# Row sums of squares from a token-major copy of the input, opening loads in another order, and products issued cell by cell

## Chip, cores and metric

One core of one Trainium2 chip runs the whole kernel. The metric is device time in microseconds (us), the median of several runs. TensorE is called PE here, VectorE DVE, ScalarE ACT, GpSimd POOL, and SyncE, which only issues transfers, SP.

## What is computed

One layer of a streaming encoder over 2048 tokens of width 1024, in float32:

```python
h = rmsnorm(x, norm_mix_pre)             # y = x * rsqrt(mean(x*x) + eps) * g
proj = h @ w_in                          # pool 512 | GLU 2*512 | gate_a 1024 | gate_b 1024
branch_a = pool_mixer(u_pool, ...)       # 4 trailing means, small maps, projection
branch_b = conformer_conv(u_glu, ...)    # GLU, depthwise conv 31, layernorm, silu, projection
merged = sigmoid(g_a) * branch_a + sigmoid(g_b) * branch_b
x = x + rmsnorm(merged @ w_o, norm_mix_post)
f = square(relu(rmsnorm(x, norm_mlp_pre) @ w_up)) @ w_down
x = x + rmsnorm(f, norm_mlp_post)
```

Only the first norm's `mean(x*x)` is computed in another way by the change; the rest is the same arithmetic in another order.

## The kernel before, in words

Activations lie channels on partitions, tokens along the row: a tile `x0[c, t]` is 128 x 1024, for 128-channel pairs c = 0..3 and a token half t = 0, 1 of a block. The 2048 tokens are two blocks b = 0, 1 of 1024. Each float32 operand is cut into a high part (an ACT cast, `wh`, `big`, L221 and L228 in the profile) and a low part (a DVE subtraction of the high part, `wl`, `big`, L122), and each product is three passes: high by high, high by low, low by high. Large products are made of smaller ones in octets with sums and differences of cells (`Octet`; the opening's first GLU octet `o1` is a `Plain`, without sums).

One **product** is 24 matmuls 128x512 into a `glu` (or `ga`, `pool`, `up`, `down`...) tile of two PSUM banks, one bank for each output half q: twelve matmuls for q = 0, then twelve for q = 1 (`product`, `matmuls`, L267 to L296). Its operands are a weight of eight 128x128 blocks and two cells of two 512-column blocks k. The opening's products are numbered P1, P2, ... here in PE's order; P1 to P4 belong to t = 0 of `o1`, P5 and P6 to `o2`, and P7 is the first that `run_first` issues behind the hand-written opening.

A scheduler orders each engine's instructions, but in the opening (`opening`, L1612 to L1688) the order is fixed by hand: `InOrder` chains the instructions of an engine as they are written, `high_priority` puts them first, and `cast_behind` names the ACT instruction behind which the casts of `o1`'s weights for t = 1 may come. The opening starts with `idle(20, ...)`, matmuls of ones whose result nobody reads. `first_half` (L829) issues the first transfers: SP's queue takes x, `load`, and ACT's takes the parameters `cst` and the first weight in halves, `store`. P1 to P4 multiply raw x times the norm's gain (`first_parts`, ACT L809 and DVE L893), since the factor 1/rms of a token can be applied behind them. `FirstNorm` finds that factor for t = 0 (`n0`) and t = 1 (`n1`): four squares on ACT (L767), three additions and a half one on DVE (L119), eight matmuls 128x1 with `inv_d` on PE (L858), eleven small DVE operations for the root (L635 to L698), eight 128x128 matmuls that spread it over partitions (`spread`, L728), and an ACT copy (L870). P5 on take normed cells, which `first_cell` (L873, two DVE operations of 0.74 us a cell, L877) makes.

For block b = 1 the same sums are made between the products of block 0 by `in_stats(1)` (L903): it loads x again, takes the squares on ACT, adds on DVE and sums with eight matmuls for each t.

Weights already loaded are kept in device memory as low parts (`kept<-wl`) and fetched again for block 1.

## Time and profile before

| | us |
|---|---|
| median of 3 runs (2153.32 to 2160.22) | 2156.2 |
| the profiled execution | 2155.09 |
| its span in the trace | 2153.0 |
| PE busy in the span | 2133.3 |
| DVE, ACT, POOL busy | 1667.3, 1040.7, 78.2 |
| start of P7 / of P13 in the span | 47.30 / 80.44 |

The span is what the profiler saw of the execution; the 2.1 us around it are launch and end. An engine's busy time divided by the span is its share; the windows view gives the same by stretches, with the clock granted to PE as a share of 2.4 GHz. In a timeline a row is a run of like instructions with the start, the time they took together and, in brackets, how long the engine stood idle before them and what released it.

### The profile page before, as it was taken

The page shows a single profiled execution, that of the slowest core. Times are in us where ns is not written, and L with a number is a line of the kernel's source. Part 1 is how long each engine was busy: PE and PEld are TensorE (multiplying, and loading weights), DVE is VectorE, ACT ScalarE, POOL GpSimd, SP SyncE. Part 2 cuts the span into 40 slices and gives each one's busy share as a digit, 9 for nine tenths or more (in the row PEclk, how much of TensorE's full clock was granted, in tenths as well). Part 3 has the DMA queues.
Part 4 walks back from the last instruction along what each step waited for, and adds up shares of the span by engine and source line. Part 5 has one row for each costly group of instructions (what it writes and reads, how often), then busy time and mean ns, then how long its engine had stood idle before and what let it go on. Part 6 is the DMA issues. An engine that isn't in the chain of part 4 may idle for free.

```text
span 2153.0 us, 25284 instructions
## 1 busy us (share of the span) xinstructions
PE 2133.3 (99%) x9582; PEld 1768.6 (82%) x9582; DVE 1667.3 (77%) x1637; ACT 1040.7 (48%) x1101; POOL 78.2 (4%) x143
## 2 busy tenths in 40 slices
PE   9999999999999999999999999999999999999998
PEld 7888888888888887888888888888888888888887
DVE  8998788997778878997868795667776657576976
ACT  6444453334543635445564684555663332234751
POOL 1000000000000000000000000000000000120002
PEclk9999999999999999999999999999999999999999
DMA  7688898778997786445697698677898997896977
GB/s 275 242 287 326 322 367 272 242 246 309 332 379 247 267 329 259 171 160 188 249 359 298 241 342 326 245 261 276 314 350 303 353 380 261 333 369 234 301 256 217
DMA packets 173929, 618.39 MB, mean 287 GB/s; under 512 B 19312, under 2 KB 21616, under 8 KB 173808
## 3 DMA queue, kind: packets, MB, share of 16 engines
q1 hardware_dynamic: 142736, 505.80, 64.6%
q0 software_dynamic: 17824, 64.07, 8.4%
q10 hardware_dynamic: 13248, 46.92, 5.5%
q8 instruction: 75, 1.23, 0.2%
q14 instruction: 46, 0.38, 0.1%
HBM read 406.89 MB, written 209.81 MB: 286 GB/s over the span
## 4 chain that ended last, share of the span: by engine, by line
PE 88%; DVE 7%; DMA 3%; issue 1%; ACT 1%; SPq 0%; ACTq 0%; DVEq 0%
PE up L271 25%; PE down L271 22%; PE gb L271 7%; PE wo L271 7%; PE ga L271 6%; PE glu L271 5%; PE rb L271 5%; PE A L271 4%; PE B L271 4%; PE pool L271 2%; DVE tr L119 1%; DVE big L122 1%; DVE y L1015 1%; DVE wl L122 1%; DVE tr L122 1%
## 5 line engine op out<-in xcount | busy, mean ns | idle before, releaser
L271 PE MATMUL up<-big,wh 128*128 128x512 f32 x1792 | 481.4, 390 | 4.6 <-DVE tr L119 3.8
L271 PEld LDWEIGHTS up<-big,wh 128*128 128x128 f32 x1792 | 336.7, 188 | 75.2 <-issue 4.2
L228 ACT CAST wh<-wr 128x1024 fp32r<-128x1024 f32 x196 | 205.9, 1051 | 349.4 <-PE up L271 101.4
L1015 DVE SCALAR_TENSOR_TENSOR y<-v,cst,y 128x1024 f32<-128x1024 f32 x240 | 307.6, 1282 | 3.0
L271 PE MATMUL down<-big,wh 128*128 128x512 f32 x872 | 294.9, 389 | 0.0
L228 ACT CAST wh<-ws 128x1024 fp32r<-128x1024 f32 x128 | 134.7, 1053 | 298.8 <-PE up L271 91.2
L271 PE MATMUL up<-big,wl 128*128 128x512 f32 x896 | 276.2, 389 | 0.0
L271 PE MATMUL down<-big,wl 128*128 128x512 f32 x688 | 212.1, 389 | 0.0
L271 PEld LDWEIGHTS up<-big,wl 128*128 128x128 f32 x896 | 168.4, 188 | 35.0
L271 PE MATMUL down<-tr,wh 128*128 128x512 f32 x504 | 196.2, 389 | 0.5 <-DVE tr L122 0.5
L122 DVE TENSOR_TENSOR wl<-ws,wh 128x1024 fp32r<-128x1024 f32 x120 | 146.6, 1221 | 58.7 <-ACT wh L228 58.4
L271 PEld LDWEIGHTS down<-big,wh 128*128 128x128 f32 x872 | 163.6, 188 | 33.9
L122 DVE TENSOR_TENSOR wl<-wr,wh 128x1024 fp32r<-128x1024 f32 (+1 forms) x121 | 146.3, 1212 | 34.7 <-ACT wh L228 33.4
L122 DVE TENSOR_TENSOR big<-big,big 128x1024 fp32r<-128x1024 f32 (+1 forms) x108 | 130.2, 1221 | 41.0 <-ACT big L1150 17.7
L122 DVE TENSOR_TENSOR tr<-tr,big 128x1024 fp32r<-128x1024 f32 x94 | 112.7, 1221 | 53.0 <-ACT big L1892 40.6
L271 PEld LDWEIGHTS down<-big,wl 128*128 128x128 f32 x688 | 129.2, 188 | 26.8
L271 PE MATMUL wo<-big,wh 128*128 128x512 f32 x480 | 128.5, 390 | 0.0
L271 PE MATMUL glu<-big,wh 128*128 128x512 f32 x464 | 125.1, 391 | 0.7 <-ACT wh L535 0.5
L271 PE MATMUL ga<-big,wh 128*128 128x512 f32 x448 | 120.0, 389 | 0.0
L271 PE MATMUL gb<-big,wh 128*128 128x512 f32 x448 | 119.9, 389 | 0.0
L1892 ACT CAST big<-tr 128x1024 fp32r<-128x1024 f32 x70 | 72.1, 1049 | 97.0 <-DMA tr<-fd 75.0
L271 PEld LDWEIGHTS down<-tr,wh 128*128 128x128 f32 x504 | 94.6, 188 | 20.5 <-DVE tr L122 1.0
(245 smaller groups left out, 3406.7 us busy)
## 6 DMA issues: line engine op xcount, KB each, us to landing
tr<-fd SPq DMA_DIRECT2D x98, 512.0 KB, 7.5
wl<-kept SPq DMA_DIRECT2D x85, 512.0 KB, 5.1
wr<-w_down SPq DMA_DIRECT2D x80, 512.0 KB, 7.8
kept<-wl SPq DMA_DIRECT2D x72, 512.0 KB, 6.1
wr<-w_up SPq DMA_DIRECT2D x64, 512.0 KB, 5.1
wr<-w_in SPq DMA_DIRECT2D x59, 512.0 KB, 5.6
fd<-tr ACTq DMA_DIRECT2D x54, 512.0 KB, 5.2
big<-fd SPq DMA_DIRECT2D x48, 512.0 KB, 6.7
```

The costliest lines, as they stand in the source:

```text
L119: return nc.vector.tensor_tensor(o, a, b, op=ALU.add)
L122: return nc.vector.tensor_tensor(o, a, b, op=ALU.subtract)
L228: nc.scalar.copy(hi[:, :n], src[:, :n])
L271: i = nc.tensor.matmul(ps, w[wp][:, (at + k) * P : (at + k + 1) * P], rhs[k][xp], start=start and n == 0, stop=stop and n == len(order) - ...
L1015: nc.vector.scalar_tensor_tensor(acc, v[:, k : k + TB], wk, acc, op0=ALU.mult, op1=ALU.add)
L1892: nc.scalar.copy(hi, t)
```

## The change

- **Sums of squares.** A second input array `xn` holds x with tokens on partitions, 128 x 1024 to a tile. ACT's Square with `accum_out` sums a token's squares along the row (`token_squares`), so neither DVE nor PE adds anything for them. The opening loads eight such tiles more; `in_stats(1)` loads `xn` in the place of `xt`.
- **Opening.** The first transfers come in another order, the first two x tiles in halves, `cst` in two parts. The idle matmuls are 9 in the place of 20, and 3 later ones are dropped. The first weight half is cast on DVE. Cells of t = 1 get their gain on ACT (two 128x512 operations) and 1/rms by one DVE multiplication. `cast_behind` names a later instruction.
- **Products.** Every product issues its 24 matmuls cell by cell: for each of the two cells four high by high, four with the low x, four with the low weight, in each four two for q = 0 and two for q = 1. The first product has a list of its own, `COMING`.

```diff
@@ constants
+STAIRS = tuple(
+    (q, 2 * c + k, wp, xp)
+    for c in (0, 1) for wp, xp in ((0, 0), (0, 1), (1, 0)) for q in (0, 1) for k in (0, 1)
+)
+COMING = ((0, 0, 0, 0), (0, 0, 1, 0), (1, 0, 0, 0), (0, 0, 0, 1), (0, 1, 0, 0), (0, 1, 1, 0))
...
-IDLE = (4, 5, 3)
+IDLE = (4, 5)
@@ product
-        rhs = cell_rhs(cells)
-        i = [matmuls(half_of(ps, q), w, 4 * q, rhs, start, stop) for q in (0, 1)]
-        mark(i[1])
+        in_order(STAIRS, ps, w, cells, start, stop)
+
+    def in_order(order, ps, w, cells, start, stop):
+
+        rhs, seen = cell_rhs(cells), set()
...
+        for n, (q, k, wp, xp) in enumerate(order):
+            i = nc.tensor.matmul(
+                half_of(ps, q), w[wp][:, (4 * q + k) * P : (4 * q + k + 1) * P], rhs[k][xp],
...
@@ Plain.by_halves, Plain.run
-                nc.scalar.copy(hi[:, s], raw[:, s])
+                (nc.scalar.copy if i else nc.vector.tensor_copy)(hi[:, s], raw[:, s])
...
+            if job == (0, 0, 0):
+                in_order(COMING, self.ps, w, cells, True, False)
@@ token_squares
+    def token_squares(st, g, x):
+
+        nc.scalar.activation(x, x, AF.Square, scale=D**-0.5, accum_out=st[:, g : g + 1])
@@ first_half
-            load_x(0, x0, ORDER_X[:1])
-            store(cst, params)
+            store(cst[:, :C_PSC], params[:, :C_PSC])
...
+            half(load, x0[0, 0], xt[0, 0, 0], 0)
+            half(store, w, w_in[0, 0], 0)
+            half(load, x0[0, 0], xt[0, 0, 0], 1)
+            half(store, w, w_in[0, 0], 1)
+            half(load, x0[1, 0], xt[0, 1, 0], 0)
+            half(load, x0[1, 0], xt[0, 1, 0], 1)
+            o.get(1)
             load_x(0, x0, ORDER_X[2:CPS])
-            for q in (1, 2, 3):
-                o.get(q)
-            load_x(0, x0, ORDER_X[CPS:])
+            o.get(2)
+            load(cst[:, C_PSC:], params[:, C_PSC:])
+            n0.load()
+            o.get(3)
@@ FirstNorm
-        def squares(self):
-            sq = Squares(TR)
...
-        def sums(self):
-            self.st = root_psum()
-            for g in range(G):
-                i = nc.tensor.matmul(
...
+        def load(self):
+            self.x, self.st = [tr() for _ in range(G)], small("st", G)
+            for g, x in enumerate(self.x):
+                load(x, xn[0, self.t, g])
+
+        def squares(self, groups):
+            for g in groups:
+                token_squares(self.st, g, self.x[g])
@@ first_cell
+        if t:
+            first_gain(c, t)
+            mul(two(x), two(x), per_token(r0[t]))
+            return x
@@ in_stats
-            sq = Squares(TR)
-            for c in range(CPS):
+            st = small("st", G)
+            for g in range(G):
                 x = tr()
-                load(x, xt[b, c, t])
+                load(x, xn[b, t, g])
                 yield 1
-                sq.add(x)
...
+                token_squares(st, g, x)
...
-            yield from inv_rms_steps([ss], inv_d, TR, 4, got)
+            yield from spread_steps(root_dve(st), TR, 4, got)
@@ opening
-        idle(20, root_psum())
+        idle(9, root_psum())
...
+            n0.squares(range(G))
...
         o1.run((0, 0, 1), None, none)
         with tc.high_priority(offset=URGENT):
-            n0.sums()
             n0.root()
             o1.prepare(1, 0, 1)
-            act()
             o2.prepare(1)
...
+            n1.load()
+            load_x(0, x0, ORDER_X[CPS:])
+            n1.squares((0, 1))
...
         o1.run((1, 0, 0), None, none)
-        idle(IDLE[2], root_psum(), marks[mybir.EngineType.PE])
         with tc.high_priority(offset=URGENT):
             n0.spread()
-            n1.sums()
             cells0(0, 0), cells0(1, 0)
-            parts.need(1)
-            n1.root()
+            for g in (2, 3):
+                parts.step()
+                n1.squares((g,))
...
         o1.run((1, 0, 1), None, none)
         with tc.high_priority(offset=URGENT):
+            n1.root()
             cells0(2, 0), cells0(3, 0)
+            parts.step()
+            o2.prepare(2)
             parts.need(2)
-            o1.cast_behind = [
...
-            o2.prepare(2)
+            first_gain(0, 1), first_gain(1, 1)
...
         o2.run(1, None, none)
         with tc.high_priority(offset=URGENT):
             n1.spread()
             cells0(0, 1), cells0(1, 1)
             parts.need(8)
+            first_gain(2, 1), first_gain(3, 1)
+            o1.cast_behind = [
...
@@ arrays
+        "xn": g["x"].reshape(NB, 2, T // P, P, D),
```

On SP the first twelve transfers are now these (`big` is x, `wr` a weight of `w_in`, `xn` the second layout, the first two rows two halves each):

```order
L137 DMA big_216<-xt 128x512 x2
L137 DMA big_217<-xt 128x512 x2
L137 DMA wr_224<-w_in 128x1024
L137 DMA big_226<-xt 128x1024
L137 DMA big_228<-xt 128x1024
L137 DMA wr_230<-w_in 128x1024
L137 DMA cst<-params 128x228
L137 DMA tr_233<-xn 128x1024
L137 DMA tr_234<-xn 128x1024
L137 DMA tr_235<-xn 128x1024
L137 DMA tr_236<-xn 128x1024
L137 DMA wr_242<-w_in 128x1024
```

Before, the queue began with four whole x tiles, three weights and the four x tiles of t = 1; these four now stand behind four more `xn` tiles, as rows 18 to 21.

On ACT in the opening, from the cast of the first cell of P6 to the cast of P7's weight; before (`wh_646` is P7's weight, `big_529` and `big_533` P6's cells, `wh_692` the weight after):

```order
L557 COPY tr_523<-glu_420 128x1024
L221 CAST big_529<-big_221 128x1024
L221 CAST big_533<-big_223 128x1024
L228 CAST wh_646<-wr_644 128x1024
L444 COPY tr_569<-glu_544 128x1024
L870 COPY r_239<-rb_571 128x512
L228 CAST wh_692<-wr_690 128x1024
L221 CAST big_585<-big_231 128x1024
L221 CAST big_589<-big_233 128x1024
```

and now (`wh_515` is P6's weight, `wh_630` P7's, `big_509` and `big_520` P6's cells, `big_397` to `big_403` the x tiles of t = 1):

```order
L230 CAST big_509<-big_226 128x1024
L237 CAST wh_515<-wr_513 128x1024
L230 CAST big_520<-big_228 128x1024
L838 ACTIVATE big_397<-big_397,cst 128x512 x2
L838 ACTIVATE big_399<-big_399,cst 128x512 x2
L466 COPY tr_553<-glu_528 128x1024
L901 COPY r_213<-rb_555 128x512
L230 CAST big_567<-big_397 128x1024
L230 CAST big_571<-big_399 128x1024
L838 ACTIVATE big_401<-big_401,cst 128x512 x2
L838 ACTIVATE big_403<-big_403,cst 128x512 x2
L237 CAST wh_630<-wr_628 128x1024
```

P7's weight was cast straight behind P6's cells; it now stands behind the eight gains of t = 1, P7's own cells `big_567` and `big_571`, and two copies.

On DVE in the up projection, ahead of the operation that frees the `up` tile whose owner PE waits for at 847.84 us; before:

```order
L119 TENSOR_TENSOR ws_6664<-wr_6658,wr_6660 128x1024
L122 TENSOR_TENSOR tr_6519<-big_5845,big_5641 128x1024
L122 TENSOR_TENSOR tr_6525<-big_5936,big_5743 128x1024
L122 TENSOR_TENSOR wl_6604<-ws_6601,wh_6603 128x1024
L122 TENSOR_TENSOR big_6522<-tr_6519,big_6521 128x1024
L122 TENSOR_TENSOR big_6528<-tr_6525,big_6527 128x1024
L1015 SCALAR_TENSOR_TENSOR y_6385<-v_5650,cst,y_6385 128x1024
L122 TENSOR_TENSOR ws_6666<-ws_6664,wr_6662 128x1024
L122 TENSOR_TENSOR wl_6669<-ws_6666,wh_6668 128x1024
L119 TENSOR_TENSOR tr_6593<-up_6481,tr_6557 128x1024
```

and now:

```order
L128 TENSOR_TENSOR ws_6624<-wr_6618,wr_6620 128x1024
L131 TENSOR_TENSOR wl_6564<-ws_6561,wh_6563 128x1024
L131 TENSOR_TENSOR tr_6479<-big_5805,big_5601 128x1024
L131 TENSOR_TENSOR tr_6485<-big_5896,big_5703 128x1024
L1057 SCALAR_TENSOR_TENSOR y_6345<-v_5610,cst,y_6345 128x1024
L131 TENSOR_TENSOR big_6482<-tr_6479,big_6481 128x1024
L131 TENSOR_TENSOR ws_6626<-ws_6624,wr_6622 128x1024
L131 TENSOR_TENSOR big_6488<-tr_6485,big_6487 128x1024
L131 TENSOR_TENSOR wl_6629<-ws_6626,wh_6628 128x1024
L128 TENSOR_TENSOR tr_6553<-up_6441,tr_6517 128x1024
```

The sum `ws_6666`, which ACT casts into `wh_6668`, stood directly ahead of `wl_6669`, which needs that cast; the same sum, `ws_6626`, now has a subtraction between it and `wl_6629`.

## Rows read from the trace of the kernel before

**Rows 1.** The page, busy us (share of the span) xinstructions of each engine.

```profile
PE 2133.3 (99%) x9582; PEld 1768.6 (82%) x9582; DVE 1667.3 (77%) x1637; ACT 1040.7 (48%) x1101; POOL 78.2 (4%) x143
```

**Rows 2.** Waits of PE: what it waited for, us in total, times, longest.

```profile
PE pool L271 <- DVE tr L119: 1.5, 2, 1.1
...
PE up L271 <- DVE big L122: 0.8, 1, 0.8
...
PE down L271 <- DVE tr L122: 0.5, 1, 0.5
```

**Rows 3.** Windows: us, busy (x) by engine, granted clock, DMA share, GB/s.

```profile
0.00:5.00 5.00, 4.01 (x11) 3.19 (x12) 0.00 (x0) 1.49 (x2) 1.21 (x10) 1.00 0.59 201
5.00:10.00 5.00, 4.47 (x19) 3.06 (x18) 3.50 (x6) 3.95 (x7) 0.00 (x0) 1.00 1.02 395
8.00:9.00 1.00, 1.00 (x5) 0.79 (x5) 1.00 (x2) 1.00 (x2) 0.00 (x0) 1.00 1.04 416
10.00:15.00 5.00, 5.00 (x24) 4.14 (x23) 4.50 (x6) 5.00 (x7) 0.87 (x2) 1.00 1.04 389
15.00:20.00 5.00, 4.41 (x21) 3.35 (x19) 4.55 (x5) 4.92 (x6) 0.38 (x1) 1.00 1.01 407
...
847.00:851.00 4.00, 3.16 (x8) 2.56 (x9) 4.00 (x4) 2.84 (x3) 0.00 (x0) 0.57 0.54 221
```

**Rows 4.** PE timeline, 0 to 95 us: start, us, operation [idle before <-releaser].

```profile
0.99 6.41 PE L610 MATMUL rb<-ones 128*128 128x512 f32 x20 [0.99 <-POOL inv_d L187]
...
19.97 1.02 PE L858 MATMUL rb<-inv_d,tr 128*128 128x1 f32 x8 [0.59 <-DVE tr L119]
...
26.42 0.85 PE L610 MATMUL rb<-ones 128*128 128x512 f32 x3
...
29.29 1.65 PE L271 MATMUL glu<-big,wh 128*128 128x512 f32 x6
...
47.30 1.52 PE L271 MATMUL glu<-big,wh 128*128 128x512 f32 x6
...
50.02 1.52 PE L271 MATMUL glu<-big,wh 128*128 128x512 f32 x6
...
80.44 1.52 PE L271 MATMUL glu<-big,wh 128*128 128x512 f32 x6
```

**Rows 5.** ACT timeline, 0 to 95 us.

```profile
9.78 2.56 ACT L809 ACTIVATE big<-big,cst 128x512 fp32r<-128x512 f32 x4
...
13.18 3.90 ACT L767 ACTIVATE tr<-big 128x1024 f32<-128x1024 f32 x4
...
22.29 1.07 ACT L767 ACTIVATE tr<-big 128x1024 f32<-128x1024 f32 x1 [0.83 <-DMA big<-xt]
...
40.54 1.04 ACT L228 CAST wh<-wr 128x1024 fp32r<-128x1024 f32 x1
41.48 1.01 ACT L444 COPY tr<-glu 128x1024 f32<-128x1024 f32 x1
42.39 0.58 ACT L870 COPY r<-rb 128x512 f32<-128x512 f32 x1
```

**Rows 6.** DVE timeline, 0 to 33 us and 834 to 850 us.

```profile
15.21 3.89 DVE L119 TENSOR_TENSOR tr<-tr,tr 128x1024 f32<-128x1024 f32 x3 [0.68 <-ACT tr L767]
...
25.40 0.15 DVE L635 TENSOR_SCALAR sa<-rb 128x4 f32<-128x4 f32 x1
...
27.48 2.36 DVE L122 TENSOR_TENSOR wl<-wr,wh 128x1024 fp32r<-128x1024 f32 x2
29.76 2.72 DVE L877 SCALAR_TENSOR_TENSOR big<-big,cst,rb 128x512 f32<-128x512 f32 x4
...
836.13 1.23 DVE L122 TENSOR_TENSOR wl<-ws,wh 128x1024 fp32r<-128x1024 f32 x1 [1.11 <-ACT wh L228]
```

**Rows 7.** PE timeline, 145 to 154 us and 842 to 852 us.

```profile
151.86 0.95 PE L599 MATMUL rb<-inv_d,tr 128*128 128x1 f32 x8
...
847.84 2.90 PE L271 MATMUL up<-big,wh 128*128 128x512 f32 x6 [3.76 <-DVE tr L119]
```

More of the change, by code (lines that the diff above doesn't have):

```diff
@@ L292, in product @@
     def product(ps, w, cells, start=True, stop=True):
-        rhs = cell_rhs(cells)
-        i = [matmuls(half_of(ps, q), w, 4 * q, rhs, start, stop) for q in (0, 1)]
-        mark(i[1])
+        in_order(STAIRS, ps, w, cells, start, stop)
+    def in_order(order, ps, w, cells, start, stop):
+        rhs, seen = cell_rhs(cells), set()
+        last = {q: n for n, (q, k, wp, xp) in enumerate(order)}
+        for n, (q, k, wp, xp) in enumerate(order):
+            i = nc.tensor.matmul(
+                half_of(ps, q), w[wp][:, (4 * q + k) * P : (4 * q + k + 1) * P], rhs[k][xp],
+                start=start and q not in seen, stop=stop and n == last[q],
+                skip_group_check=True,
+            )
+            if not seen:
+                ordered(i)
+            seen.add(q)
+        mark(i)
     def half_of(ps, q):
@@ L549, in run @@
                 self.ps = psum(self.lab)
-            product(self.ps, w, cells, start=k == 0, stop=k == 1)
+            if job == (0, 0, 0):
+                in_order(COMING, self.ps, w, cells, True, False)
+            else:
+                product(self.ps, w, cells, start=k == 0, stop=k == 1)
             flush()
@@ L804, in block_kernel, with gained @@
     ORDER_X = tuple((c, t) for t in (0, 1) for c in (0, 1, 2, 3))
-    def gained(dst, src, gain, c):
-        for i in (0, 1):
+    def gained(dst, src, gain, c, halves=(0, 1)):
+        for i in halves:
             s = slice(i * T, (i + 1) * T)
@@ L829, in first_half, with half @@
     def first_half(o):
+        def half(queue, dst, src, i):
+            queue(dst[:, i * T : (i + 1) * T], src[:, i * T : (i + 1) * T])
         with tc.high_priority(offset=URGENT):
-            load_x(0, x0, ORDER_X[:1])
-            store(cst, params)
+            store(cst[:, :C_PSC], params[:, :C_PSC])
             o.raw[0] = w = mk(p_wr, "wr")
-            store(w[:, :T], w_in[0, 0, :, :T])
-            load_x(0, x0, ORDER_X[1:2])
-            store(w[:, T:], w_in[0, 0, :, T:])
+            for c, t in ORDER_X[:2]:
+                x0[c, t] = mk(*BIG)
+            half(load, x0[0, 0], xt[0, 0, 0], 0)
[5 more added lines that the diff above has]
+            o.get(1)
             load_x(0, x0, ORDER_X[2:CPS])
-            for q in (1, 2, 3):
-                o.get(q)
-            load_x(0, x0, ORDER_X[CPS:])
+            o.get(2)
+            load(cst[:, C_PSC:], params[:, C_PSC:])
+            n0.load()
+            o.get(3)
     class FirstNorm:
@@ L847, in __init__ @@
             self.t, self.r = t, r[:, t * T : (t + 1) * T]
[L849 to L863 removed]
+        def load(self):
[5 more added lines that the diff above has]
+                token_squares(self.st, g, self.x[g])
         def root(self):
[L866 removed]
+            self.dg = spread_dve(root_dve(self.st), None)
         def spread(self):
@@ L871, in spread, with first_gain @@
             r0[self.t] = rb if self.t == 0 else self.r
+    gained_x = set()
+    def first_gain(c, t):
+        if (c, t) not in gained_x:
+            gained_x.add((c, t))
+            gained(x0[c, t], x0[c, t], C_PRE, c)
     def first_cell(c, t):
         x = x0[c, t]
+        if t:
+            first_gain(c, t)
+            mul(two(x), two(x), per_token(r0[t]))
+            return x
         for i in (0, 1):
@@ L888, in first_parts @@
                 hi, lo = mk(*BIG, F32R), mk(*BIG, F32R)
-                with tc.high_priority(offset=URGENT):
-                    gained(hi, x0[c, 0], C_PRE, c)
-                    for i in (0, 1):
+                for i in (0, 1):
+                    with tc.high_priority(offset=URGENT):
+                        gained(hi, x0[c, 0], C_PRE, c, (i,))
                         s = slice(i * T, (i + 1) * T)
@@ L1611, in block_kernel @@
     o1, o2 = glu(0, parts)
-    first_half(o1)
     r = mk(p_ss, "r", F32, (P, W))[:, :TB]
     n0, n1 = (FirstNorm(t, r) for t in (0, 1))
+    first_half(o1)
     dve = InOrder(mybir.EngineType.DVE)
     def opening():
-        act = InOrder(mybir.EngineType.Activation)
-        idle(20, root_psum())
+        fix = InOrder(mybir.EngineType.DVE, mybir.EngineType.Activation)
+        idle(9, root_psum())
         with tc.high_priority(offset=URGENT):
             halves = o1.by_halves(0, 0, 0)
+            next(halves)
             parts.step()
@@ L1626, in opening @@
             drain(halves)
+            o1.prepare(0, 0, 1)
             parts.need(("u", 1))
-            o1.prepare(0, 0, 1)
-            n0.squares()
             o1.prepare(1, 0, 0)
-            n1.squares()
-        dve()
+            n0.squares(range(G))
+        fix()
         o1.run((0, 0, 0), None, none)
@@ L1665, in opening @@
             parts.need(8)
-        dve()
+            first_gain(2, 1), first_gain(3, 1)
+            o1.cast_behind = [
+                i for i in nc.cur_bb.bb.instructions if i.engine == mybir.EngineType.Activation
+            ][-1]
+        fix()
         o2.run(2, None, none)
-        dve.skip()
+        fix.skip()
         with tc.high_priority(offset=URGENT):
@@ L1671, in opening @@
             parts.need(3)
-        dve()
+        fix()
+        dve.last.update(fix.last)
     opening()
```

27 lines of the change are left out of this document (10 added, 17 removed).

## The prediction

> **What bounds the kernel now.** I read the page first: PE is busy for 2133.3 of a span of 2153.0 us [rows 1], so only work taken off PE, or one of the 20 us in which it stands still, can shorten the run. The waits of PE come next: beside 3.76 us at 847.84 for a DVE operation [rows 7], they are 1.5 us in two places ahead of `pool` products (1.1 and 0.44), 0.8 and 0.5 [rows 2]. Then the timeline of the opening, where the change is. PE does 20 idle matmuls to 7.40, eight sums of one column at 19.97 behind a wait of 0.59, and from 26.42 to 29.29, for 2.87 us, idle matmuls, the spread and the second sums instead of a product. P7 starts at 47.30, P13 at 80.44 [rows 4]. A half product of twelve matmuls takes 50.02 - 47.30 = 2.72 us, 0.227 each, so 5.44 a product. The opening is judged by one number: when P12 ends, 80.44 before.
>
> **The opening, step by step.** I replayed it by hand along each engine's new order, with durations from rows. On ACT, start to start (a row's last instruction overlaps the next by about 0.1): a cast 41.48 - 40.54 = 0.94, a copy 42.39 - 41.48 = 0.91, the copy of 1/rms 0.58 - 0.1, a square (3.90 - 0.1)/4 = 0.95, a gain of half a tile (2.56 - 0.1)/4 = 0.62 [rows 5]. On DVE: a whole tile (2.36 - 0.1)/2 = 1.13, a normed half cell 2.72/4 = 0.68, the root 27.48 - 25.40 = 2.1 [rows 6].
>
> Removed: on DVE the additions, twice about 4.5 us (3.89 for three, and a half one) [rows 6]; on PE the sums, twice 0.9, and three idle matmuls. The DVE time alone buys nothing here, unless PE waits for DVE. The idle matmuls at the start took 6.41 for 20, 1.7 above 20 x 0.227 + 0.16: some eight of them ran at half pace [rows 4]. Nine may therefore leave P1 to begin at half pace. Costed at nothing: P4 waits 1.85 us anyway, below, and P7 more; without that cover it would be up to 1.7.
>
> Added: `xn`. Up to the fourth `xn` tile, 7.2 MB must land. The windows moved 201, 395, 389 and 407 GB/s in their 5 us [rows 3], 6.96 MB by 20 us, so 7.2 MB have moved at 20.6; landing comes about 1.0 later, as the last x tile of before (7.46 MB, 21.2 by the same sum) released its square at 22.29 [rows 5]. So 21.6. Its square ends at 22.7, the root at 25.0, spread done and **P4 starts at 25.9**, 3.4 earlier than the 29.29 of before, behind a wait of 1.85. P5 runs 31.4 to 36.8. The four squares of `n1` stand on ACT behind casts and end at 32.8; the root at 35.35; the next cells on DVE (0.68 a half) reach 36.8. On SP, P4's weight now stands behind the four `xn` tiles; its cast ends at 24.8, still ahead of P4. P6's stands behind the last x tiles and lands at 37.5, as ACT comes to it. POOL's stores of low parts stay where they were. From 36.8 ACT has no gap: two casts of cells and one of P6's weight (2.8), four half gains (2.5), two copies (1.4) end at 43.6. P6 waits 1.1 for its weight's cast and runs 38.85 to 44.3. DVE's first t = 1 cell is ready at 44.9; two casts of the first two such cells, four half gains and the cast of `wh_630` end at 50.5.
>
> **So P7 waits about 6.3 us and starts at 50.55, against 47.30.** Before, this cast stood at 40.54, 7 us ahead of its product [rows 5]; now it stands behind the last gain, because `cast_behind` moved. From P7 on nothing waits in the replay, while before lost 0.5 in small waits between P7 and P13: P12 ends at 50.55 + 6 x 5.44 = 83.2, **+2.75 us**. Bounds: with `xn` 6 us earlier the ACT chain alone puts the end at 79.96, -0.5; each us that it lands later adds a whole us.
>
> **PE's clock behind that wait.** In this trace a stop of 3.76 us was followed by a granted clock of 0.57 in the next four us, the lower of two levels (1.2 of 2.4 GHz) for most of it, and the first six matmuls took 2.90 where six take 1.52 [rows 3, 4, 7]. A stop of 6.3 costs the same by that row: **+1.4**, between 0 and twice that.
>
> **Block 1's sums.** The eight one-column matmuls at 151.86 (0.95 us), and eight more like them later, leave PE [rows 7]: **-1.9**. Some 9 us of additions on DVE go too, as many as in the opening, in stretches where PE does not wait for it; ACT keeps its squares, and the load is one for one: nothing.
>
> **Product order.** 24 matmuls stay 24 matmuls. Where PE waited for the low part of the second cell, needed as sixth or seventh matmul and now as seventeenth, there are ten matmuls more, 2.3 us: the waits of 0.8 and 0.5 go, **-1.3** [rows 2]. The first of the `pool` waits (0.44) stands behind `in_stats`' additions on DVE, which are gone: **-0.4** [rows 2]; the other stays. Whether a change of PSUM bank after every two matmuls costs, no row shows by itself; halves meet once a product now and 0.227 holds across them [rows 4]: nothing, with rival C for more.
>
> **The wait at 847.84.** DVE works there without a gap from 836.13, where it waited 1.11 us for an ACT cast [rows 6]. In the new order the sum that ACT casts stands one operation further ahead, 1.13, which covers that 1.11: **-1.1**. Then 2.7 remain, and the clock may or may not fall behind them: 1.4 to the range, not to the sum.
>
> **Sum:** 2.75 + 1.4 - 1.9 - 0.4 - 1.3 - 1.1 = -0.55 us. The profiled execution took 2155.09, of which 2153.0 is span and 2.1 lies around it; it stands 1.1 below the median of 2156.2. So 2154.5 by its own time, and **2155.6** against the median.
>
> **Rivals.**
>
> *A, faster: the relief of DVE and PE is paid out.* DVE loses 18 us of additions in the first 250; if the later order slips into place, the waits of 3.76, 1.1 and the clock behind the first go too. Beside the -1.1 and the -0.4 taken, that is 2.7 + 1.1 + 1.4 = 5.2. With the opening at its shortest (-0.5 for 2.75, or -3.2) the time is 2155.6 - 5.2 - 3.2 = 2147.2. For: PE waits there for DVE alone. Against: one of these waits stands 700 us behind the last DVE operation removed, and the order shows one place mended. The halves of this rival come singly, too: 2150.4 and 2152.4.
>
> *B, slower: `xn` lands late.* The opening moves 4.2 MB more, its first tiles in more pieces. Each us that the fourth tile is late moves P4, the ACT chain and P7 by one: from 0.6 us late the sum has turned to slower, from 7.1 us a measurement sees it. Against it stands the row from 8 to 9 us, 416 GB/s with a weight's half tile between whole ones [rows 3]: pieces of 256 KB did not slow the queue. Priced by a fixed cost of the size of ACT's landing lag above, 1.0 for each of three extra transfers and as much again for their wait in the queues, 6 us: 2155.6 + 6 = 2161.6. The Trainium skill, "DMA: Bandwidth & Descriptors", section "Rules for kernel authors", advises at least 1 MiB per DMA for full bandwidth, and its section on the anatomy of a DMA gives some 2 us fixed for each; three more transfers by that rule would also come to 6 us, if nothing overlapped. By that rule the halves are a loss; the trace's row speaks against it, as it does with tiles of 512 KB at 389 to 416 GB/s.
>
> *C, slower: the bank change costs.* The new order changes the PSUM bank twelve times a product, ten more than before. There are about 375 products among 9582 matmuls [rows 1]. The rows' last digit is 10 ns, so a change could hide some 5: 10 x 375 x 5 ns = 19 us, 2174.6. From 7.1 us on, 1.9 ns a change, this decides the sign. Against: the step from one half to the other shows nothing.
>
> *D: the change does not do what it says,* since the ACT casts are ready sooner than replayed or the wait at P7 is filled: then the opening is even, and with the clock kept the time is 2155.6 - 2.75 - 1.4 = 2151.4.
>
> **Chances.** What a measurement of this kernel can tell from no change is 0.3%, 6.5 us, so 2149.7 and 2162.7 are the bounds. My forecast, with the bounds of the clock and the small waits, 0.45; D 0.16 and the single halves of A 0.10, within it or near; A whole 0.13; B 0.09, about half of it beyond 2162.7; C 0.07. A whole and some of D and the halves that run together give faster 0.20; C, half of B and what I have not seen give slower 0.16; 0.64 for the same. The range reaches to A's 2147.2 and B's 2161.6 with a us at either end for the scatter of a median: 2146 to 2163, which leaves out C and the tails.
>
> **What would show it.** In the new trace: no one-column matmul with `inv_d` in the first 250 us; PE standing still for 5 to 7 us before P7, released by an ACT cast of a weight, and a granted clock below 1 behind it; P4 near 26 and P13 near 83; about 2.7 in place of 3.76 near 843; the waits for low parts gone; 0.227 between the starts of matmuls throughout. I am wrong if P7 starts before 48 (the chain on ACT is not the limit), if the fourth `xn` tile's square starts behind 24 (B), if twelve matmuls take more than 2.74 (C), or if new waits of DVE's stand where none stood.

## The result, and the profile after

The change makes the kernel slower: 2167.4 us, median of 4 runs (2163.96 to 2168.74), against 2155.9, median of 4 (2153.32 to 2160.22). The ratio is 1.0048, with a 95% interval of 1.0032 to 1.0064. The forecast was 2155.6 in 2146 to 2163.

| | before | after |
|---|---|---|
| the profiled execution, us | 2155.09 | 2163.96 |
| its span | 2153.0 | 2162.2 |
| start of P7 / of P13 | 47.30 / 80.44 | 52.14 / 87.74 |
| start of the first `pool` product | 91.32 | 98.62 |
| from there to the end of the span | 2061.7 | 2063.6 |

The page of the changed kernel answers to [rows 1]: PE is busy 1.1 us less, and the span is 9.2 longer.

```profile
PE 2132.2 (99%) x9536; PEld 1766.6 (82%) x9536; DVE 1650.7 (76%) x1618; ACT 1046.5 (48%) x1124; POOL 78.2 (4%) x143
```

The timeline of PE in the opening (start, us, operation, count, and in brackets the idle time before and what ended it), beside [rows 4]:

```profile
0.99 4.21 PE L639 MATMUL rb<-ones 128*128 128x512 f32 x9 [0.99 <-POOL ones L194]
6.09 0.76 PE L310 MATMUL glu<-big,wh 128*128 128x512 f32 x1 [0.90 <-DVE wh L557]
...
8.50 1.65 PE L310 MATMUL glu<-big,wh 128*128 128x512 f32 x3 [0.98 <-ACT wh L557]
...
27.86 2.03 PE L310 MATMUL glu<-big,wh 128*128 128x512 f32 x8
...
52.14 3.78 PE L310 MATMUL glu<-big,wh 128*128 128x512 f32 x8 [5.94 <-ACT wh L237]
...
57.43 2.37 PE L310 MATMUL glu<-big,wh 128*128 128x512 f32 x8
...
87.74 1.98 PE L310 MATMUL glu<-big,wh 128*128 128x512 f32 x8
```

P4 starts at 27.86, 1.4 us earlier than before, and P7 at 52.14, 4.8 later. The matmuls of P1 stand up to 0.43 us apart, until 13.4, where 0.227 is the pace. P7 follows a stop of 5.94 us for the cast of its weight, as forecast (6.3), and its first half takes 57.43 - 52.14 = 5.29 where 2.72 is the pace. The windows (us, busy time by engine, granted clock, DMA share, GB/s) show the clock behind that stop, as [rows 3] did behind 847 us:

```profile
10.00:15.00 5.00, 5.00 (x16) 3.95 (x15) 4.92 (x7) 4.63 (x7) 0.75 (x2) 1.00 1.04 406
...
52.00:60.00 8.00, 7.86 (x22) 6.25 (x23) 8.00 (x9) 7.78 (x10) 0.00 (x0) 0.61 0.60 195
```

For the slow matmuls of P1 the first of these windows reads 1.00. That is no measurement: in this trace the record of the clock begins at 13.86 us, and the view counts time without a record as 1.00. In a second trace of the same kernel (e13 below) the record begins earlier, and shows the lower level, 1.2 GHz, for the same matmuls:

```profile
10.00:12.00 2.00, 2.00 (x6) 1.61 (x5) 1.92 (x4) 2.00 (x3) 0.49 (x1) 0.50 1.03 410
```

On ACT, the square of the fourth `xn` tile at 21.59, the copy of 1/rms at 28.62, the gains at 48.60, and the weight's cast behind them at 51.06 (two casts, P7's the first):

```profile
21.59 1.06 ACT L631 ACTIVATE tr<-tr 128x1024 f32<-128x1024 f32 x1 [0.46 <-DMA tr<-xn]
...
28.62 0.57 ACT L901 COPY r<-rb 128x512 f32<-128x512 f32 x1
...
46.45 2.24 ACT L230 CAST big<-big 128x1024 fp32r<-128x1024 f32 x2 [1.29 <-DVE big L134]
48.60 2.56 ACT L838 ACTIVATE big<-big,cst 128x512 f32<-128x512 f32 x4
51.06 1.98 ACT L237 CAST wh<-wr 128x1024 fp32r<-128x1024 f32 x2
```

On DVE the root of n0 begins at 22.77; the normed cells wait 1.85 us more for ACT's copy at 28.62:

```profile
22.77 0.17 DVE L664 TENSOR_SCALAR sa<-st 128x4 f32<-128x4 f32 x1 [6.49 <-ACT tr L631]
...
29.22 2.72 DVE L919 SCALAR_TENSOR_TENSOR big<-big,cst,rb 128x512 f32<-128x512 f32 x4 [1.85 <-ACT r L901]
```

The waits of PE over the whole kernel (us in total, times, longest), which answer to [rows 2]. The waits for low parts (0.8 and 0.5) are gone, as are the one at 146 us and 1.35 of the 3.76 at 844 (now 2.41 at 854.6). The `pool` wait near 390 has grown from 1.1 to 1.6, and others stand where none stood: `gb` for ACT, `up` for an ACT activation, `down` for weight casts, `B`.

```profile
PE glu L310 <- ACT wh L237: 6.6, 2, 5.9
PE up L310 <- DVE tr L128: 3.4, 2, 2.4
PE down L310 <- ACT wh L237: 2.0, 2, 1.4
PE pool L310 <- DVE tr L128: 1.6, 1, 1.6
PE up L310 <- ACT tr L1560: 1.2, 1, 1.2
...
PE gb L310 <- ACT tr L466: 0.9, 1, 0.9
...
PE B L280 <- DVE big L131: 0.8, 1, 0.8
```

### The profile page after: what moved, and what is told of

Its sections match the earlier page's. It is cut to its first block, busy times and chain, and to the rows that moved or that the text cites. A ratio compares the mean times of both kernels' runs of the same rounds, so it can differ in the third digit from the quotient of the medians.

```text
span 2162.2 us, 25192 instructions
## 1 busy us (share of the span) xinstructions
PE 2132.2 (99%) x9536; PEld 1766.6 (82%) x9536; DVE 1650.7 (76%) x1618; ACT 1046.5 (48%) x1124; POOL 78.2 (4%) x143
## 4 chain that ended last, share of the span: by engine, by line
PE 86%; DMA 6%; DVE 5%; ACT 1%; issue 1%; SPq 0%; DVEq 0%; ACTq 0%
PE up L310 24%; PE down L310 21%; PE ga L310 7%; PE glu L310 5%; PE gb L310 5%; PE A L280 4%; PE wo L280 4%; PE B L280 4%; PE rb L310 4%; PE wo L310 3%; PE pool L310 3%; DMA tr<-yd 2%; DVE y L1057 1%; PE down L280 1%; DMA tr<-fd 1%
## 5 line engine op out<-in xcount | busy, mean ns | idle before, releaser
L310 PE MATMUL up<-big,wh 128*128 128x512 f32 x1792 | 444.1, 390 | 4.5 <-DVE tr L128 3.4
L310 PE MATMUL up<-big,wl 128*128 128x512 f32 x896 | 239.8, 390 | 0.0
L310 PE MATMUL down<-big,wh 128*128 128x512 f32 x872 | 226.5, 390 | 2.0 <-ACT wh L237 2.0
L310 PE MATMUL down<-big,wl 128*128 128x512 f32 x688 | 184.1, 390 | 0.0
L310 PE MATMUL down<-tr,wh 128*128 128x512 f32 x504 | 134.8, 390 | 0.0
L310 PE MATMUL glu<-big,wh 128*128 128x512 f32 x464 | 120.2, 401 | 8.4 <-ACT wh L237 6.6
L310 PEld LDWEIGHTS glu<-big,wh 128*128 128x128 f32 x464 | 89.5, 194 | 28.9 <-ACT wh L237 7.1
L310 PE MATMUL gb<-big,wh 128*128 128x512 f32 x448 | 111.2, 390 | 1.1 <-ACT tr L466 0.9
L310 PE MATMUL ga<-big,wh 128*128 128x512 f32 x448 | 110.7, 390 | 0.0
```

The lines of the kernel that those rows point to most:

```text
L310: i = nc.tensor.matmul(half_of(ps, q), w[wp][:, (4 * q + k) * P : (4 * q + k + 1) * P], rhs[k][xp], start=start and q not in seen, stop=st ...
```

## The experiments

All but the last two are edits of one of the two kernels. The table gives the median, the ratio to the kernel before in the same comparison with its interval, and two numbers of each run's profiled execution: by how much the first `pool` product starts later than the 91.32 of before (**opening**), and how long the span goes on from there (**rest**, 2061.7 before).

| run | median | ratio (interval) | opening | rest |
|---|---|---|---|---|
| the change | 2167.4 | 1.0048 (1.0032 to 1.0064) | +7.3 | 2063.6 |
| e1, P7's weight ahead | 2162.7 | 1.0037 (1.0024 to 1.0049) | +3.0 | 2064.7 |
| e2, 20 idle matmuls | 2164.3 | 1.0040 (1.0027 to 1.0052) | +6.1 | 2065.2 |
| e3, both | 2160.3 | 1.0022 (1.0013 to 1.0032) | +3.1 | 2061.6 |
| e4, old product order | 2161.6 | 1.0025 (1.0016 to 1.0035) | +6.6 | 2060.0 |
| e5, before, cell order | 2160.5 | 1.0020 (1.0010 to 1.0031) | -0.2 | 2062.9 |
| e6, before, block 1's sums | 2153.5 | 0.9978 (0.9968 to 0.9988) | +0.3 | 2057.4 |
| e7, e3 with old order | 2155.4 | 0.9997 (0.9987 to 1.0006) | +4.2 | 2057.9 |
| e8, e7, copy ahead | 2158.2 | 1.0003 (0.9994 to 1.0013) | +3.6 | 2060.0 |
| e9, e5, late high weight | 2157.1 | 1.0001 (0.9992 to 1.0010) | -0.3 | 2064.5 |
| e10, e9 and e6 | 2155.1 | 0.9997 (0.9987 to 1.0006) | -0.5 | 2062.9 |
| e11, e8, no second xn | 2156.7 | 1.0004 (0.9993 to 1.0015) | +2.2 | 2060.6 |
| e12, opening alone | 2164.3 | 1.0032 (1.0022 to 1.0041) | +7.5 | 2060.6 |
| e13, the change again | 2165.1 | 1.0037 (1.0021 to 1.0053) | +7.0 | 2066.2 |
| e14, e5 again | 2160.4 | 1.0019 (1.0008 to 1.0029) | -0.1 | 2065.7 |

### The opening: e1, e2, e3

e1:

```diff
             cells0(0, 1), cells0(1, 1)
+            o1.prepare(0, 1, 0)
             parts.need(8)
```

> The changed kernel with one line more: P7's weight is cast on ACT right ahead of P7's own cells instead of behind the last gain. Theory W (the wait of 5.94 us at P7 comes from the place of that cast, and the low clock behind it, 13 matmuls and some 3 us, from the wait): P7 starts at 47.6 to 48.5 instead of 52.14, the clock does not fall behind it, P13 starts near 80.8 instead of 87.74, and the time falls by about 7 us, to 2160. Rival X (ACT has too much work there, and the cast's place only decides which product waits): P8 or P9 waits in P7's place, P13 moves by less than 3 us, and the time falls by 0 to 3.

```profile
40.77 2.12 PE L310 MATMUL glu<-big,wh 128*128 128x512 f32 x8 [1.20 <-ACT wh L237]
...
47.89 1.21 PE L310 MATMUL glu<-big,wh 128*128 128x512 f32 x4 [1.37 <-ACT big L230]
50.22 1.20 PE L310 MATMUL glu<-big,wh 128*128 128x512 f32 x4 [1.11 <-DVE big L131]
```

The stop of 5.94 us became two of 1.37 and 1.11, PE keeps its pace behind them, and the opening gives back 4.3 of its 7.3 us. W holds for that much, not for the 7 us expected: P7 now waits for its own cells, whose chain runs late, and P8 stands still for another 1.02 us, until 57.03, for a low part of DVE's.

e2:

```diff
-        idle(9, root_psum())
+        idle(20, root_psum())
```

> The changed kernel with 20 idle matmuls at the start instead of 9. Theory I (nine leave P1 at the lower clock, P1 ends 3.8 us late, and the spread of 1/rms stands behind P3 on PE, so the whole chain to P7 starts late): P1 starts at 7.4 and its matmuls stand 0.227 apart, P4 starts at 25.9 instead of 27.86, bounded by the root of n0 at 24.9, P7 near 50.3 with its wait of some 6 us unchanged, time 1.5 to 2 us less. Rival Y (P1 is bound by its loads and casts, the clock only fills the gaps): P4 moves by less than 0.5 and the time stays.

```profile
0.99 6.25 PE L639 MATMUL rb<-ones 128*128 128x512 f32 x20 [0.99 <-POOL ones L194]
7.09 0.40 PE L310 MATMUL glu<-big,wh 128*128 128x512 f32 x1
...
25.61 0.30 PE L757 MATMUL rb<-ident,sp 128*128 128x128 f32 x1 [0.83 <-DVE sp L727]
...
52.43 3.43 PE L310 MATMUL glu<-big,wh 128*128 128x512 f32 x8 [4.37 <-ACT wh L237]
```

P1's matmuls now keep their pace and the spread begins at 25.61 instead of 27.01, P4 at 26.55 instead of 27.86, so I is right on the clock, and Y, which had P4 stay, is not. But P7 starts at 52.43, no earlier than with nine. The 1.2 us that the opening gains come from a shorter low-clock stretch behind P7's stop. What stands between the spread and P7 is the copy of 1/rms, which ACT does behind two squares of t = 1 at 28.91 here, at 28.62 in the change.

e3 has both edits.

> The two edits of the runs before together. Theories W and I: they add up, P13 starts near 79, earlier than the 80.44 of the kernel before, and the time is some 9 us below the changed kernel, 2158.5: what is then left above the kernel before is waits behind the opening. Rivals X or Y: no more than the better of the two alone.

The opening stays at +3.1, that of e1 alone: the edits do not add, though W and I said that they would. P7 starts at 47.77, as in e1 (47.89), and behind its two stops, 1.35 and 1.14 us, the granted clock from 50 to 53.5 us is 0.51 in this trace; behind e1's two, 1.37 and 1.11, it stays at 1.00. The median is 2.4 below that of e1, but the intervals overlap.

### The product order: e4, e5, e9, e10

e4 (`product` as before; `COMING` stays for the first):

```diff
-        in_order(STAIRS, ps, w, cells, start, stop)
+        rhs = cell_rhs(cells)
+        i = [matmuls(half_of(ps, q), w, 4 * q, rhs, start, stop) for q in (0, 1)]
+        mark(i[1])
```

> The changed kernel with the products of before, output half by half, and only the first product in its new order. Theory S (the cell by cell order costs nothing by itself, and the new waits behind the opening come from the scheduler's other order on DVE and ACT): a half product of twelve takes 2.72 us in both, the waits of 0.8 and 0.5 for low parts come back, the opening is the same, time within 3 us of the changed kernel. Rival T (the new order makes the waits, since both halves of a PSUM tile now end together and its eviction is needed sooner): the waits near 554, 606, 1081 and 1751 us go, and the time falls by 3 to 5 us.

The waits of PE:

```profile
PE glu L280 <- ACT wh L237: 4.4, 1, 4.4
PE up L280 <- DVE tr L128: 4.1, 2, 3.2
...
PE up L280 <- DVE big L131: 0.8, 1, 0.8
...
PE down L280 <- DVE tr L131: 0.5, 1, 0.5
```

The time is rival T's: 5.8 us less than the change in the medians (3.5 less than those of its second measurement, e13), and, in the profiles, 3.6 less behind the opening. T's reason, that both halves of a PSUM tile now end together, was not tested. The waits of `gb`, `B` and `down` on ACT are gone, and those for low parts are back.

The cause is not on PE, whose pace is the same in both. The scheduler orders all engines' work together, so another order of the matmuls gives another order there too, over the whole program: the change and e4 differ at 78 places among the 996 instructions of SP, at 131 on DVE and at 68 on ACT (an instruction that moves counts as two). One place, on SP near 585 us in the change:

```profile
585.64 0.33 SPq L137 DMA_DIRECT2D wr<-w_in  x1
586.06 0.40 SPq L137 DMA_DIRECT2D tr<-yd  x1
```

and in e4:

```profile
582.66 0.41 SPq L137 DMA_DIRECT2D tr<-yd  x1
584.34 0.33 SPq L137 DMA_DIRECT2D wr<-w_in  x1
```

In cell order a high weight is used for the last time as 20th matmul of a product, in the old order as 23rd; here the load of a later weight (`wr<-w_in`) stands ahead of a load of `yd` in the change, and behind it in e4. DVE waits for that `yd` in the change:

```profile
594.61 1.22 DVE L134 TENSOR_TENSOR tr<-tr,r 128x1024 f32<-128x1024 f32 x1 [1.27 <-DMA tr<-yd]
```

In e4 this step does not wait, though the one before it waited 0.51 us for a `yd`:

```profile
589.95 1.22 DVE L134 TENSOR_TENSOR tr<-tr,r 128x1024 f32<-128x1024 f32 x1
```

On ACT a later step of the same chain waits for DVE in the change, and the copy that frees a `gb` tile stands behind them:

```profile
603.12 1.24 ACT L1122 ACTIVATE tr<-tr,cst 128x1024 f32<-128x1024 f32 x1 [2.88 <-DVE tr L134]
...
606.48 1.00 ACT L466 COPY tr<-gb 128x1024 f32<-128x1024 f32 x1
```

PE waits 0.92 us for that copy, at 607.53 (the row `gb` among the waits above); in e4 the products there run through, but for 0.25.

That is how a place in SP's queue can reach PE, but it does not show that the order of these two loads makes the wait. In e13, the same kernel with the same order, DVE does not wait for that `yd`, and PE's wait at this product is 0.3:

```profile
594.17 1.23 DVE L134 TENSOR_TENSOR tr<-tr,r 128x1024 f32<-128x1024 f32 x1
```

And in e7 (below), which has the old product order and the `yd` ahead, DVE waits longer for it, and PE has the same wait at `gb`:

```profile
588.83 1.23 DVE L134 TENSOR_TENSOR tr<-tr,r 128x1024 f32<-128x1024 f32 x1 [1.58 <-DMA tr<-yd]
```

```profile
PE gb L280 <- ACT tr L468: 0.9, 1, 0.9
```

The waits that stand in every trace with the change's cell order, and in none with the old one, are other ones: `down` and `up` for ACT. Their sizes are given behind e14.

e5 puts the cell order into the kernel before. (With it goes one more thing: the old code ties the first matmul of each half to the product before, the new code only that of the product. All runs in cell order share this, and none tests it apart.)

```diff
-        i = [matmuls(half_of(ps, q), w, 4 * q, rhs, start, stop) for q in (0, 1)]
+        in_order(STAIRS, ps, w, cells, start, stop)
```

> The kernel before, with all its products issued cell by cell and nothing else. From the run with the old order in the changed kernel (5.8 us less, with the very same order of instructions on DVE, ACT and SP), theory T: the order itself loses. A high weight is used for the last time three matmuls earlier, 0.69 us, so its successor's cast and load come earlier and meet other transfers; waits appear at evictions and weight casts (gb, up, B, down), some 5 to 6 us, and the low-part waits of 0.8 and 0.5 go. Expected: 3 to 6 us above before, 2158.6 to 2161.6. Rival S2 (the order loses only on top of the other changes, which moved the same transfers): within 1.5 us of before, or 1.3 below it.

Slower by 1.0020 (1.0010 to 1.0031), some 4 us, as T has it and against S2. What the expectation says of "the very same order" was wrong: e5 and the kernel before differ at 87 places on SP, 130 on DVE and 72 on ACT, and the load of `w_in` near 585 us stands ahead of that of `yd` here too. The `gb`, `up` and `down` waits stand at the same products as in the change:

```profile
PE down L305 <- ACT wh L232: 2.5, 2, 1.3
...
PE up L305 <- ACT tr L1535: 1.2, 1, 1.2
```

e9 moves the last use of the high weight back to the 23rd place:

```diff
+STAIRS = STAIRS[:18] + ((1, 2, 0, 1), (0, 2, 1, 0), (0, 3, 1, 0), (1, 2, 1, 0), (1, 3, 0, 1), (1, 3, 1, 0))
```

> The kernel before with products cell by cell as in the run before of that kind, but the last eight matmuls of each product in another order: the high weight is used until the last but one, as in the old order, the low weight last. Theory T, narrow (the early release of the high weight, 0.69 us, is what draws casts and loads forward and makes the waits): the waits near 602, 1074, 1737 and 1744 us go, those for low parts stay away, time at or up to 1.3 below before, 2154.3 to 2156. Rival T2 (the release of the cells' parts, 8 to 12 matmuls earlier, or the place of the low weight does it): the waits stay, and the time is 3 to 5 us above before, 2160.

The median falls by 3.4 us against e5, to 1.3 above that of the kernel before (ratio 1.0001): near T's narrow range, and not T2's 2160. SP now differs from before at 33 places, DVE at 52, and the load of `yd` near 585 us is ahead again. But in the one profile PE still waits near 600 (for another chain: DVE stood 3.01 us for a load `wl<-kept` at 577), 1738 and 1746, and only the wait near 1074 is gone. The one near 848 is back at 3.6 (1.1 in e5), and the rest is no shorter than in e5's profile. That one was of e5's fastest execution, 4.4 below its median; e14's rest is 2065.7, and e9's profile stands at its median. So the order of the last six matmuls, with the late use of the high weight, has a part in it by the medians, and takes away the wait near 1074; those of `down` stay.

e10 is e9 and e6 together.

> The kernel before with block 1's sums from the second layout and with that later high weight. By theory T, narrow: 1 us below the run with the sums alone, 2152.4. By T2: 3 to 5 above it, 2157.

2155.1, between T's 2152.4 and T2's 2157, with a rest of 2062.9 against e6's 2057.4. The parts do not add: e9 alone is level with the kernel before, and yet on top of e6 the same order takes back most of what block 1's sums gain. The intervals of e10 and e6 just meet, so this is less certain than e5.

### Block 1's sums: e6

```diff
-            sq = Squares(TR)
-            for c in range(CPS):
+            st = small("st", G)
+            for g in range(G):
                 x = tr()
-                load(x, xt[b, c, t])
+                load(x, xn[b, t, g])
                 yield 1
-                sq.add(x)
+                token_squares(st, g, x)
...
-            yield from inv_rms_steps([ss], inv_d, TR, 4, got)
+            yield from spread_steps(root_dve(st), TR, 4, got)
```

> The kernel before, with block 1's sums of squares from the second layout on ACT and nothing else. Theory B1: two times eight one-column matmuls leave PE (1.9 us) and the wait of 0.44 before the pool product at 146 goes, 2.3 us in all: 2153.3; the waits behind stay about where they were (1.1 at 389, 3.8 at 844). Rival: the DVE operations that fall away let the rest slip, and the waits at 389 or 844 change by more than 1 us either way.

The `pool` product that waited 0.44 before starts without a wait, 0.35 earlier than before in spite of an opening 0.25 later:

```profile
145.97 1.52 PE L272 MATMUL pool<-big,wh 128*128 128x512 f32 x6
```

Where the `A` products begin, at 294.07 against 296.51, the kernel is 2.4 us ahead, so it has gained 2.7 since the opening; by the end it is 4.0 ahead in the profile, 3.5 in the medians. The waits at 389 and 844 go from 1.1 to 0.8 and from 3.8 to 3.1, less than the rival's 1 us each: B1, with more gained than its 2.3. This version beats both kernels, by 0.9978 (0.9968 to 0.9988) the one before.

### What is left of the opening: e7, e8, e11, e12

e7 is e3 with the old product order.

> The changed kernel with the old product order, P7's weight cast ahead of its cells, and 20 idle matmuls. If the edits add: 4 us less than the changed kernel with the old order alone, 2157.6; P13 starts 2.5 to 3.1 us later than before, since the chain behind the spread still starts late. Rival: with the old product order, which needs the low part of the second cell as sixth matmul, P6 and P7 wait for low parts, and less than 2 us are gained.

2155.4, level with the kernel before and 2 us better than expected, 6.2 below e4. The opening is at +4.2, later than the 2.5 to 3.1 expected, since with the old order P6 and P7 wait for low parts (4.5 us of waits `glu` for DVE in all). So the rival has the waits right and the gain wrong.

e8:

```diff
-            n1.squares((0, 1))
         fix()
         o1.run((1, 0, 0), None, none)
         with tc.high_priority(offset=URGENT):
             n0.spread()
+            n1.squares((0, 1))
```

> As the run before, and on ACT the copy of 1/rms for t = 0 stands ahead of the first two squares of t = 1 instead of behind them. Theory R (in the changed kernel and in the run with 20 idle matmuls DVE's first normed cell waits until that copy, at 28.6 and 28.8, though the spread is done at 26.6 or so; the two squares wait for their transfers): the copy comes at 26.7 to 27.2, DVE's cells near 27.3 instead of 29.4, P6 and P7 some 1.5 to 2 us earlier, no lower clock behind P7, P13 within 1.5 us of before, and the time is 2 to 3 us less than in the run before. Rival L (the second four xn tiles and the weights behind them bound P6 and P7 anyway): P6 moves by less than 0.5.

ACT and DVE:

```profile
26.73 0.59 ACT L903 COPY r<-rb 128x512 f32<-128x512 f32 x1 [0.36 <-PE rb L759]
...
39.09 1.04 ACT L237 CAST wh<-wr 128x1024 fp32r<-128x1024 f32 x1 [0.94 <-DMA wr<-w_in]
```

```profile
27.94 2.72 DVE L921 SCALAR_TENSOR_TENSOR big<-big,cst,rb 128x512 f32<-128x512 f32 x4
```

The copy comes at 26.73 and the cells at 27.94, 1.6 earlier than e7's chain (29.52): R is right there. But the cast of P6's weight now waits for its load, 0.94 us, P6 starts at 40.19 instead of 40.72, and the opening gains 0.6 only: that is L. In the medians nothing is gained (2158.2 against 2155.4; the intervals, around 1.0003 and 0.9997, overlap).

e11:

```diff
-            n1.load()
+            n1.x, n1.st = n0.x, small("st", G)
```

> As the run with the copy of 1/rms ahead, but the four xn tiles of t = 1 are not loaded: the squares for t = 1 are taken of the tiles of t = 0 (which leaves the sums of t = 1 out of the computation). 2.1 MB less stand ahead of P6's weight. Rival L, whole (these loads make the 3.6 us by which P13 starts late): P6 starts near 38 and P13 within 0.5 of before. Theory M (the chain of ACT and DVE from the spread on bounds P6 and P7, and the load only P6's weight, by the 0.94 that ACT waited for it): P6 starts at 39.2 instead of 40.2, P13 1 to 1.5 earlier, still 2 to 2.6 us behind before.

```profile
38.94 1.65 PE L280 MATMUL glu<-big,wh 128*128 128x512 f32 x5
41.65 0.51 PE L280 MATMUL glu<-big,wh 128*128 128x512 f32 x1 [1.06 <-DVE big L131]
```

P6 starts at 38.94 and the opening falls from +3.6 to +2.2: theory M, the loads are 1.4 us of it. What the 2.2 that are left consist of was not tested further; PE's waits there are for DVE, as P6's stop at 41.65 for a low part (`glu` for DVE, 4.3 us in all).

e12 has the opening alone (e4's product order, `in_stats` as before).

> The opening of the changed kernel alone: the old product order (but for the first product) and the old sums for block 1. If the parts add: the changed kernel is 11.5 above before, the product order makes 3.5 to 5.8 of it and block 1's sums -3.5, so the opening alone 9 to 11, at 2165 to 2167; by its profile P13 starts 6.5 to 7.3 late and the rest is clock and waits behind. Rival (the opening costs what it shows up to P13, and no more): 2162.5 to 2164.

8.6 us above before by the medians, 6.2 by the profiled executions: the opening shows +7.5 at the first `pool` product and takes 1.1 back behind it. The time lies just above the rival's 2164, and below the 2165 of parts that add.

### The same kernel twice: e13, e14

> The changed kernel as it is, for a second profile. Its first profile was of the fastest of four executions (2163.96, mean clock 0.997); the others took 2167 to 2169 at 0.994 and 0.995. Theory Q (the same waits stand in every execution, and in the slower ones the clock falls behind more of them): in a profile at 0.994 to 0.995, some 15 to 25 more matmuls stand 0.427 apart, behind the waits at 393, 606, 852 or 1751 us, the waits themselves within 0.5 of the first profile. Rival (the waits themselves differ from one execution to the next): their sum is 3 us larger and the number of slow matmuls about the same.

Its waits:

```profile
PE down L310 <- ACT wh L237: 2.6, 2, 1.7
...
PE up L310 <- DVE tr L128: 1.5, 1, 1.5
PE rb L624 <- DVE tr L128: 1.5, 1, 1.5
PE B L280 <- ACT big L1192: 1.2, 1, 1.2
```

> The kernel before with products cell by cell, for a second profile: the first was of its fastest execution (2156.12, clock 0.999), 4.4 below its median. Theory Q: at a time near 2160, the waits as in the first profile and the clock fallen behind two to four of them, 15 to 25 slow matmuls more. Rival: longer waits.

Theory Q fell. The second profile of the change has 29 matmuls at half pace where the first has 32, and that of e5 10 and 7. The gaps between matmuls above 0.3 us, apart from those, come to 3.1 us more in e13 and 2.6 more in e14. The waits come back at the same products (`gb`, `up` for an activation of 1.2, `down` near 1747 and 1755), but a wait is 0.3 us in one execution and 0.9 in another, and some stand in one alone (`B` 1.2, `rb` 1.5 in e13). Why was not followed for each; at the `gb` of 607 us it was a transfer, the `yd` above, that DVE waited for in one execution and not in the other.

The column "rest" shows the order's price best, since it holds each kernel's waits behind the opening. Five profiles with the cell order and block 1's new sums have 2061.6 to 2066.2, five with the old order and the same sums 2057.4 to 2060.6. The means are 2064.3 and 2059.2: 5.1 us.

PE's waits in the same ten traces account for it. By how much the starts of matmuls stand further apart than 0.227 us, where they are more than 0.3 apart and not at half pace, comes to 15.6 us behind the first `pool` product in the mean of the five with the cell order, and to 10.0 in the other five:

| waiting products, and for whom | cell order | old order |
|---|---|---|
| `down`, for weight casts on ACT (old order: for DVE) | 2.6 | 0.7 |
| `gb`, for ACT | 2.0 | 0.3 |
| `B` | 1.5 | 0.1 |
| `pool`, for DVE | 1.9 | 0.7 |
| `up`, for an activation on ACT | 1.3 | 0 |
| `up`, for DVE | 2.2 | 4.5 |

So the order does not only cost: it shortens `up`'s waits for DVE, the one near 844 us above all (1.1 in e5, where the kernel before has 3.8). The `up` wait for ACT stands in all seven traces with the change's order and not in e9 and e10, so it hangs on the order of a product's last six matmuls. The `down` waits for ACT stand in all nine, those two among them. What in the order makes these, and those of `gb`, `B` and `pool`, stays open.

## Why the prediction was wrong

**Product order, the term that failed.** The prediction said "24 matmuls stay 24 matmuls" and took 1.3 us off for low parts. Those waits did go. What it left out is that a product's order also sets when its weights and cells come free, and by that the order of SP's, DVE's and ACT's work in the whole program. The order of the changed kernel could be read beforehand; I compared it in the opening and at the wait near 844 us, and not in the rest of the program, where the 87 places on SP are (in e5 the first is at 177 us). The term was some +5 (e4 and the rests; 4 in e5) where -1.3 was put. That the order is what costs, and that it costs in waits of PE for ACT and DVE, is shown; which part of the order makes a wait is shown for the `up` wait of 1.3 alone (e9). The sign that the prediction named for being wrong, new waits of DVE's, did come (0.94 at 819 us, 0.8 at `B`). Rival C had the right sign and a wrong mechanism: a half product, twelve matmuls, takes 2.72 us in both orders.

**The stop at P7, right in place and cause.** 5.94 us measured, 6.3 forecast, and e1 shows the cast's place as the cause. P7 was put at 50.55 and came at 52.14, since the replay let DVE begin the normed cells straight behind the spread; DVE waits for ACT's copy, which stands behind two squares (e8).

**The clock behind it, under-sized.** +1.4 was put, from six matmuls behind the shorter stop of 3.76; 13 matmuls stood at half pace behind this one and the two halves took 3.0 us more. The bound of twice 1.4 just missed it. The opening came to +7.3 (7.0 in e13), not 2.75 + 1.4: of the 3.15 missing, 1.6 are P7's later start and 1.6 the clock.

**The first idle matmuls, right for P7 only.** They cost P1 its pace. The wait of 1.85 put at P4 did not cover that: P4 was put at 25.9 and came at 27.86, behind no wait, of which e2 gives back 1.3. At P7 the cover held: with 20 of them it starts no earlier. That P7's stretch at the lower clock is shorter in e2, by 1.2 us in the opening, no term had; whether the idle matmuls make it is not shown.

**Block 1's sums, right and a little small.** -1.9 and -0.4 were put; 2.7 were gained by 296 us, 3.5 in the medians (e6).

**The wait at 844, right in size, and no term of its own.** It belongs to the product order: with the old one it is 1.9 to 3.5 in the changed kernel's variants, and the cell order alone makes it 1.1 (e5). -1.1 was put, 3.76 became 2.41 and the clock held; 0.94 stands at 819 instead, and `up` waits 1.15 at 1083. In the long stretch of `up` products from 794.93 to 1108.69 the change stands 6.89 us behind at the start and 6.93 at the end.

**`xn` and rival B.** The root of n0 ended at 24.92, forecast 25.0: the opening's loads land as summed. The halves move before 10 us, where the windows fell from 201 and 395 GB/s to 172 and 368; by 20 us all but 0.13 MB of that is made up, and no run changes the halves alone, so what they cost is not shown. The advice of the Trainium skill, "DMA: Bandwidth & Descriptors", section "Rules for kernel authors", to keep a DMA at 1 MiB or more did not decide here: with whole tiles of 512 KB the windows from 10 to 15 us moved 389 GB/s before and 406 now. The 2 us that the prediction takes from the Trainium skill's section on the anatomy of a DMA stand there for transfers issued from GpSimd, and SP issues these; B's price did not rest on them.

So the parts are: the opening 7.3, the product order some 5, block 1's sums -3.5, 8.8 in all. The change was measured twice, at 11.5 above the kernel before and, in e13, at 9.0. The 2.7 by which the parts fall short of the first is about what the two measurements differ by, so no further part is shown.

## To carry to other kernels

When the matmuls of a product are put in another order, write down for each operand the place of its first and of its last use, and then compare the queue of the loads and the other engines over the whole program, not only around the change: here a weight that came free three matmuls earlier put a later load ahead of one that was needed sooner, in one of 87 places. When an instruction is put behind new work on a busy engine, follow the engine that needs its result up to the next product; here one cast behind two casts of cells and four more gains cost 4.3 us. Test the parts of such a change apart: one of three was worth 3.5 us, and was hidden under the other two.

## What was not expected of the hardware

The same 24 matmuls in another order, at the same pace of 2.72 us per twelve, moved the time by some 5 us, in waits of PE for ACT and DVE (e4, e5). Two executions of the same program on the same data differ by 3 us in their waits with about the same number of slow matmuls (e13, e14). Behind two stops of 1.4 and 1.1 us PE kept its clock in one run (e1) and lost it for some 3 us in another (e3). And a window that reads a granted clock of 1.00 at the start may hold no record of the clock at all: look at the spacing of the matmuls too.
